# Ten Strassen pairs of feed-forward blocks, token differences by GpSimd, and the last product by token halves with the final norm between

## The chip, the cores and the metric

The kernel runs on one NeuronCore of a Trainium2 chip. TensorE (PE) multiplies, VectorE (DVE) and ScalarE (ACT) do elementwise work and may read PSUM, GpSimd (POOL) does elementwise work between SBUF tiles, and SyncE's queue (SP) issues nearly all DMAs. The engines run at the same time, each takes its own instructions in a fixed order, and they wait for one another through semaphores. The metric is device time in microseconds (us), the median of several executions; one more execution was taken with the hardware profiler, and all the rows below come from it.

## The reference

A trunk of two layers over 640 tokens (512 of a prompt, 8 x 16 of samples), width 1024. Each layer adds to the residual `x` a mixer (pooling and differential attention in layer 0, an RWKV-7 recurrence in layer 1), a cross attention, and a feed-forward block. Only the feed-forward block and the last norm are touched here:

```python
def swiglu(h, wg, wu, wd):
    return (jax.nn.silu(h @ wg) * (h @ wu)) @ wd
# in each layer
h = rmsnorm(x, P['norm_ffn_g'][l])
x = x + swiglu(h, P['ffn_wg'][l], P['ffn_wu'][l], P['ffn_wd'][l])
# after both layers
y = rmsnorm(x, P['final_norm_g'])
```

`wg` and `wu` are 1024 x 2816, `wd` is 2816 x 1024.

## The kernel before

The residual lies with the width on the partitions: eight tiles `x[0..7]` of 128 x 640. An fp32 product is made of three matmuls on split operands: `split` (L216) rounds a tile to a high part (a cast on ScalarE) and takes the low part as the difference (a subtraction on VectorE, out of the source and the high part), and high x high, high x low and low x high are added up in PSUM. Every weight goes the same way: a DMA brings it into a raw tile (`wr` in `load_w`, `wraw` in `strassen`), ScalarE casts it to `wh`, VectorE makes `wl`. There are two tiles `wr` and three each of `wh` and `wl`. All elementwise helpers are single lines (`tt` is L211, `stt` L214, `mm` L230), so the profile tells instructions apart by their tiles.

The 2816 hidden columns are 22 blocks of 128. One block of gate and up takes 2 weights x 8 contraction blocks x 3 terms x 2 halves of 320 tokens = 96 matmuls of 320 columns. `ffn` (L1036) does blocks 0 and 1 straight from `x` (`un`, the tokens' factor `rstd` is multiplied in behind PSUM). While they run it makes the normed tiles `ys` (`xf` in the profile), and their splits `hl` (`xn`). Blocks 2 and 3 are computed from `hl` as whole products; during them VectorE makes, in place, the token differences of Strassen's scheme between the left half `L` and the right half `R` of the tokens (16 subtractions of 128 x 320 in `ys`) and their splits: `c` (`xc`: T2 and T4), `d` (`xd`: T3), and T1, which goes into the right halves of `hl[0..3]`. Then `wd` for blocks 0 to 3, and three groups of six blocks, each of three Strassen pairs and a `wd` product of six blocks.

`strassen` (L1126) computes two blocks with seven products of 24 matmuls, 168 in place of 192. It loads four raw weight tiles (A11, A12, A21, A22), makes S1, S2 and two differences in place (the rows `wraw<-wraw`), and splits seven of them. Products are accumulated in PSUM banks `p_a` (0 to 3) and `p_b` (4 to 7), which the blocks before it also used.

`final` (L2012) comes behind the last `wd` product. For each of five tiles of 128 tokens it transposes eight tiles of `x` into two banks, squares them with row sums on ScalarE, makes the factor, multiplies on VectorE and writes out.

The order of the instructions on each engine is set when the program is built, by a scheduler that plays the program through a timeline of its own: an instruction written later can stand ahead of an earlier one, and the semaphore waits follow from that order.

Of the kernel before, what the change touches and what calls it, by code (L numbers as in the profile page):

```python
# [9 lines left out]
F32 = mybir.dt.float32  # L10
F32R = mybir.dt.float32r
AF = mybir.ActivationFunctionType
ALU = mybir.AluOpType
# [4 lines left out]
D = 1024  # L18
# [3 lines left out]
NT = NP + NB * TS  # L22
NF = 22
HALVES = ((0, 320), (320, 320))
# [15 lines left out]
class Trunk:  # L40
# [995 lines left out]
    def ffn(self, l):  # L1036


        nc, io = self.nc, self.io
        self.banks(g=(0, 1, 2, 3, 4, 5), r=(6, 7))  # L1040
        wg, wu, wd = io["ffn_wg"][l], io["ffn_wu"][l], io["ffn_wd"][l]
        gcol = self.col["norm_ffn_g"][:, 8 * l:8 * l + 8]
        un = self.normed(gcol)
        first = [[self.load_w(self.wview(w, 0, 8, 0, 128), 8, 128)] for w in (wg, wu)]
        _, rstd = self.rms("r")
        r0 = rstd[0]
        L, R = slice(0, 320), slice(320, 640)

        hida = self.hl(2, "hid")
        with self.scope():  # L1050
            for f in range(2):
                sg, pr = self.t("sgate", 1)[:, 0:NT], self.t("gate")[:, 0:NT]

                def ev_g(m, pts):
                    for p, (t0, n) in zip(pts, HALVES):
                        self.tt(sg[:, t0:t0 + n], p, r0[:, t0:t0 + n])
                        self.act(sg[:, t0:t0 + n], sg[:, t0:t0 + n], AF.Silu)

                def ev_u(m, pts):
                    for p, (t0, n) in zip(pts, HALVES):  # L1060
                        self.tt(pr[:, t0:t0 + n], p, r0[:, t0:t0 + n])
                    self.tt(pr, pr, sg)
                    self.split(hida[f], pr)

                self.gemm(un, wg, 128, ev_g, c0=f * 128, first=() if f else first[0])
                self.gemm(un, wu, 128, ev_u, c0=f * 128, first=() if f else first[1])
                if f == 0:
                    ys = self.blocks(8, "xf")
                    hl = self.hl(8, "xn")
                    for k in range(8):  # L1070
                        self.stt(ys[k], self.x[k], gcol[:, k:k + 1], r0)
                        self.split(hl[k], ys[k])
        self.give(un, rstd)
        hidb = self.hl(2, "hid")
        c, d = self.hl(4, "xc"), self.hl(2, "xd")
        with self.scope():

            for k in range(4):
                y1, y2 = ys[k], ys[4 + k]
                self.tt(y1[:, L], y1[:, R], y1[:, L], ALU.subtract)  # L1080
                self.tt(y1[:, R], y2[:, R], y1[:, R], ALU.subtract)
                self.tt(y2[:, R], y2[:, R], y1[:, L], ALU.subtract)
                self.tt(y2[:, L], y2[:, L], y2[:, R], ALU.subtract)
                self.split(c[k], y2)
                self.split([t[:, (L, R)[k % 2]] for t in d[k // 2]], y1[:, R])
            for f in (2, 3):
                sg, pr = self.t("sgate", 1)[:, 0:NT], self.t("gate")[:, 0:NT]

                def ev_g(m, pts):
                    for p, (t0, n) in zip(pts, HALVES):  # L1090
                        self.act(sg[:, t0:t0 + n], p, AF.Silu)

                def ev_u(m, pts):
                    for p, (t0, n) in zip(pts, HALVES):
                        self.tt(pr[:, t0:t0 + n], p, sg[:, t0:t0 + n])
                    self.split(hidb[f - 2], pr)
# [7 lines left out]
        self.give(hida, hidb)  # L1104
        part = lambda h, s: (h[0][:, s], h[1][:, s])
        rhs = dict(B11=[part(hl[k], L) for k in range(4)], T1=[part(hl[k], R) for k in range(4)],
                   B21=[part(hl[4 + k], L) for k in range(4)], B22=[part(hl[4 + k], R) for k in range(4)],
                   T2=[part(c[k], R) for k in range(4)], T3=[part(d[k // 2], (L, R)[k % 2]) for k in range(4)],
                   T4=[part(c[k], L) for k in range(4)])
        for f0, nf in ((4, 6), (10, 6), (16, 6)):  # L1110
            self.banks(a=(0, 1, 2, 3), b=(4, 5, 6, 7), g=(4, 5, 6, 7), r=(6, 7))
            hid = self.hl(nf, "hid")

            at = dict(A11=0, A21=1, A22=2, A12=3, S1=4, S2=5)
            with self.scope():
                for f in range(0, nf, 2):
                    self.strassen(wg, wu, f0 + f, rhs, hid[f:f + 2], at)
                    at = dict(A21=at["A11"], A22=at["S2"], A11=at["S1"], A12=at["A21"], S1=at["A12"], S2=at["A22"])
            if f0 == 16:
                self.give(hl, c, d)  # L1120
                if l == 0:
                    self.mem = self.mem_parts("r")
            self.gemm(hid, wd, 1024, self.add_x, r0=f0 * 128)
            self.give(hid)

    def strassen(self, wg, wu, f, rhs, hid, at):  # L1126

# [881 lines left out]
            self.tt(o, p[:, 0:nch * 64], o)  # L2009


    def final(self):  # L2012
        nc, io = self.nc, self.io
        with self.scope():
            gb = [self.t("gb")[:, 0:512] for _ in range(2)]
            for g in range(2):
                nc.sync.dma_start(out=gb[g], in_=io["final_norm_g"][g * 512:(g + 1) * 512].partition_broadcast(128))
            for i in range(5):
                dst = io["y_prompt"][0, i * 128:(i + 1) * 128, :] if i < 4 else io["y_sample"].rearrange("b t d -> (b t) d")
                pg = []  # L2020
                ss = self.s("fss", 2)
                for g in range(2):
                    p = self.ps()
                    for j in range(4):
                        self.tr(p[:, j * 128:(j + 1) * 128], self.x[g * 4 + j][:, i * 128:(i + 1) * 128], 128)
                    pg.append(p)
                    sq = self.t("fsq")[:, 0:512]
                    self.act(sq, p, AF.Square, accum=ss[:, g:g + 1])
                rt = self.s("frt")
                self.tt(rt, ss[:, 0:1], ss[:, 1:2], ALU.add)  # L2030
                self.act(rt, rt, AF.Sqrt, scale=1.0 / D, bias=self.epsc[:, 0:1])
                nc.vector.reciprocal(rt, rt)
                for g in range(2):
                    y = self.t("y", 4)[:, 0:512]
                    self.stt(y, pg[g], rt, gb[g])
                    nc.sync.dma_start(out=dst[:, g * 512:(g + 1) * 512], in_=y)

    def run(self):
        self.banks(g=range(8))
        self.memd = [(self.dr.tile([128, 8, 256], F32, name=f"memk{l}"), self.dr.tile([128, 2, 1024], F32, name=f"memv{l}")) for l in range(2)]  # L2040
        self.load_x()
        with self.scope():
            self.constants()
        self.turn_x()
        self.even()
        self.cross(0)
        self.ffn(0)
        self.rwkv()
        self.cross(1)
        self.ffn(1)  # L2050
        self.final()


INS = ['x_prompt', 'x_sample', 'cache_diff_k', 'cache_diff_v', 'state_pool', 'state_rw_shift', 'state_rw_wkv',
# [33 lines left out]
```

## Time and profile before

| | |
|---|---|
| median of 3 runs | 2333.88 us (2332.62 to 2336.47) |
| the profiled execution, its own time | 2334.3 us |
| its span, first to last instruction | 2332.5 us |
| granted TensorE clock, mean over the span | 0.961 of full speed |
| busy: PE, DVE, ACT, POOL | 2204.8, 1407.1, 978.8, 338.2 us |

Busy time is the time in which an engine has at least one instruction under way. Matmuls overlap, so a matmul that the profile shows as 309 ns long may follow the last one after less than half of that: what a row of matmuls costs is the length of the stretch that they fill, divided by their number. The clock is given as a share of full speed: 1.00 is 2.4 GHz and 0.50 is 1.2 GHz.

### The profile page before, as it was taken

What the parts mean: (1) busy time and instruction counts of PE and PEld (TensorE: products, weight loads), DVE (VectorE), ACT (ScalarE), POOL (GpSimd) and SP (SyncE); (2) the same over time, 40 slices, a digit from 0 to 9 for tenths busy, and PEclk for the clock granted to TensorE, in tenths of its full rate; (3) what the DMA queues carried; (4) which work ended last, traced back from release to release, by engine and by line L of the source; (5) the groups of instructions that cost most, each with busy time, mean ns of one, the idle gap of its engine ahead of it and who ended that gap; (6) DMA issues with size and microseconds to landing.
All of it is one profiled execution on the core that took longest, in us unless ns stands there. A gap on an engine that the chain in (4) does not pass through costs nothing. (4 is left out here: it accounts for less than half of the span.)

```text
span 2332.5 us, 45975 instructions
## 1 busy us (share of the span) xinstructions
PE 2204.8 (95%) x18781; PEld 2054.9 (88%) x18781; DVE 1407.1 (60%) x2403; ACT 978.8 (42%) x1917; POOL 338.2 (14%) x392
## 2 busy tenths in 40 slices
PE   7999899999999999998998987888999999999997
PEld 7886799888999999998887886666998899999997
DVE  4458443456775656576668977457534596757573
ACT  4335432334443434456755352356323353525252
POOL 0113120002000000135452111223200110000000
PEclk8999999999999999999998887798999999999999
DMA  5228554532123232354237677674345222323222
GB/s 157 82 68 277 168 159 154 164 118 73 55 73 91 74 90 73 108 176 123 80 90 182 168 178 185 181 212 132 115 133 172 76 86 64 100 64 100 73 64 73
DMA packets 428483, 280.43 MB, mean 120 GB/s; under 512 B 79289, under 2 KB 383694, under 8 KB 428273
## 3 DMA queue, kind: packets, MB, share of 16 engines
q1 hardware_dynamic: 424673, 268.01, 39.6%
q0 software_dynamic: 3600, 9.49, 1.2%
q8 instruction: 148, 2.42, 0.4%
q14 instruction: 62, 0.51, 0.1%
HBM read 231.22 MB, written 46.20 MB: 119 GB/s over the span
## 5 line engine op out<-in xcount | busy, mean ns | idle before, releaser
L247 ACT CAST wh<-wr 128x1024 fp32r<-128x1024 f32 (+3 forms) x223 | 199.9, 898 | 459.1 <-PE p_g L230 370.6
L230 PE MATMUL p_g<-xn,wh 128*128 128x320 f32 x1408 | 291.4, 314 | 1.4 <-DVE xn L214 0.7
L230 PE MATMUL p_g<-hid,wh 128*128 128x320 f32 x1408 | 267.7, 309 | 0.8 <-DVE memhl L211 0.8
L211 DVE TENSOR_TENSOR x<-x,p_g 128x320 f32<-128x320 f32 x224 | 99.6, 483 | 238.3 <-PE p_g L230 238.0
L211 DVE TENSOR_TENSOR wl<-wr,wh 128x1024 fp32r<-128x1024 f32 (+2 forms) x195 | 204.2, 1048 | 62.1 <-ACT wh L247 49.1
L230 PEld LDWEIGHTS p_g<-xn,wh 128*128 128x128 f32 x1408 | 228.4, 190 | 10.7 <-issue 8.4
L230 PEld LDWEIGHTS p_g<-hid,wh 128*128 128x128 f32 x1408 | 221.8, 188 | 1.3 <-DVE memhl L211 1.0
L211 DVE TENSOR_TENSOR wl<-wraw,wh 128x1024 fp32r<-128x1024 f32 x126 | 154.1, 1223 | 108.1 <-ACT wh L220 90.6
L220 ACT CAST wh<-wraw 128x1024 fp32r<-128x1024 f32 x126 | 132.5, 1051 | 164.8 <-PE p_a L230 79.7
L230 PE MATMUL p_a<-xn,wh 128*128 128x320 f32 x864 | 191.3, 309 | 0.0
L230 PE MATMUL p_g<-xn,wl 128*128 128x320 f32 x704 | 182.7, 313 | 4.5 <-DVE wl L211 4.5
L230 PE MATMUL p_g<-hid,wl 128*128 128x320 f32 x704 | 163.2, 309 | 0.0
L230 PEld LDWEIGHTS p_a<-xn,wh 128*128 128x128 f32 x864 | 144.8, 188 | 0.0
L230 PE MATMUL p_g<-mixr,wh 128*128 128x320 f32 (+2 forms) x640 | 133.4, 317 | 7.9 <-ACT mv L198 3.6
L230 PE MATMUL p_a<-xn,wl 128*128 128x320 f32 x432 | 133.0, 309 | 0.0
L230 PEld LDWEIGHTS p_g<-xn,wl 128*128 128x128 f32 x704 | 123.6, 190 | 8.4 <-DVE wl L211 4.9
L230 PEld LDWEIGHTS p_g<-hid,wl 128*128 128x128 f32 x704 | 118.5, 188 | 0.0
L230 PE MATMUL p_g<-xohl,wh 128*128 128x320 f32 x512 | 111.5, 323 | 6.7 <-ACT xohl L220 6.6
L230 PEld LDWEIGHTS p_g<-mixr,wh 128*128 128x128 f32 (+2 forms) x640 | 101.1, 182 | 17.4 <-issue 5.4
L230 PEld LDWEIGHTS p_g<-xohl,wh 128*128 128x128 f32 x512 | 84.6, 193 | 10.4 <-ACT xohl L220 8.9
L211 DVE TENSOR_TENSOR wraw<-wraw 128x1024 f32<-128x1024 f32 x72 | 87.4, 1221 | 1.0
L230 PE MATMUL p_g<-mixr,wl 128*128 128x320 f32 (+2 forms) x320 | 82.0, 317 | 0.0
(532 smaller groups left out, 4976.1 us busy)
## 6 DMA issues: line engine op xcount, KB each, us to landing
wraw<-in_ffn_wg SPq DMA_DIRECT2D x72, 256.0 KB
wraw<-in_ffn_wu SPq DMA_DIRECT2D x72, 256.0 KB
wr<-in_ffn_wd SPq DMA_DIRECT2D x48, 384.0 KB
kc<-in_cache_mem_k SPq DMA_DIRECT2D x64, 256.0 KB
vc<-in_cache_mem_v SPq DMA_DIRECT2D x64, 256.0 KB
wr<-in_ev_w_in SPq DMA_DIRECT2D x16, 512.0 KB
wr<-in_xa_wk SPq DMA_DIRECT2D x16, 512.0 KB
vc<-in_cache_diff_v SPq DMA_DIRECT2D x32, 256.0 KB
```

The lines of the kernel that those rows point to most:

```text
L211: (eng or self.nc.vector).tensor_tensor(out, a, b, op=op)
L220: self.nc.scalar.copy(hi, src)
L230: self.nc.tensor.matmul(out, lhsT, rhs, start=start, stop=stop, **kw)
L247: nc.scalar.copy(wh[0:rows, 0:n], wr[0:rows, 0:n])
```

## The change

- Ten pairs: the whole products of blocks 2 and 3 are gone, and these blocks are the first Strassen pair. The groups are now blocks 0 to 5 (0 and 1 as before, two pairs), 6 to 11, 12 to 17 and 18 to 21 (two pairs), each with its `wd` product: 6, 6, 6 and 4 blocks in place of 4, 6, 6 and 6.
- The 16 token differences of a layer go to GpSimd (`sub`, with `eng=nc.gpsimd`), and the splits of `c` are made by halves of 320 columns. `hl[0..3]` get only their left halves at first.
- In layer 1 the last `wd` product (4 blocks) is `last_down`: its weights are split once into 16 tiles (`wd` in the rows) and kept, the product is made for tokens 0 to 383, all eight output tiles, and then for tokens 384 to 639. The final norm of token tiles 0, 1 and 2 stands between the output tiles of the second pass, that of tiles 3 and 4 behind it. It has four banks of its own (`p_o`), and `final` becomes `final_gain` and `final_tile`.

```diff
@@ ffn
                     for k in range(8):
                         self.stt(ys[k], self.x[k], gcol[:, k:k + 1], r0)
-                        self.split(hl[k], ys[k])
+                        self.split([t[:, L] for t in hl[k]] if k < 4 else hl[k], ys[k][:, L] if k < 4 else ys[k])
...
-            for k in range(4):
-                y1, y2 = ys[k], ys[4 + k]
-                self.tt(y1[:, L], y1[:, R], y1[:, L], ALU.subtract)
-                self.tt(y1[:, R], y2[:, R], y1[:, R], ALU.subtract)
-                self.tt(y2[:, R], y2[:, R], y1[:, L], ALU.subtract)
-                self.tt(y2[:, L], y2[:, L], y2[:, R], ALU.subtract)
-                self.split(c[k], y2)
-                self.split([t[:, (L, R)[k % 2]] for t in d[k // 2]], y1[:, R])
-            for f in (2, 3):
...
-                self.gemm(hl, wg, 128, ev_g, c0=f * 128)
-                self.gemm(hl, wu, 128, ev_u, c0=f * 128)
+        sub = lambda o, a, b: self.tt(o, a, b, ALU.subtract, eng=nc.gpsimd)
+        for k in range(4):
+            y1, y2 = ys[k], ys[4 + k]
+            sub(y1[:, L], y1[:, R], y1[:, L])
+            sub(y1[:, R], y2[:, R], y1[:, R])
+            sub(y2[:, R], y2[:, R], y1[:, L])
+            self.split([t[:, R] for t in c[k]], y2[:, R])
         for k in range(4):
             self.split((hl[k][0][:, R], hl[k][1][:, R]), ys[k][:, L])
+        for k in range(4):
+            y1, y2 = ys[k], ys[4 + k]
+            sub(y2[:, L], y2[:, L], y2[:, R])
+            self.split([t[:, (L, R)[k % 2]] for t in d[k // 2]], y1[:, R])
+            self.split([t[:, L] for t in c[k]], y2[:, L])
         self.give(ys)
-        self.gemm(hida + hidb, wd, 1024, self.add_x)
...
-        for f0, nf in ((4, 6), (10, 6), (16, 6)):
+        for f0, nf in ((0, 6), (6, 6), (12, 6), (18, 4)):
...
+            done = hida if f0 == 0 else []
+            new = self.hl(nf - len(done), "hid")
+            hid = done + new
...
+                if l == 1:
+                    self.last_down(hid, wd, f0)
+                    return
+    def last_down(self, hid, wd, f0):
+        nc = self.nc
+        self.banks(g=(4, 5, 6, 7), o=(0, 1, 2, 3))
+        nb = len(hid)
+        ws = [self.take(2, "wd", dt=F32R) for _ in range(8)]
...
+            def half(m, t0, n):
+                p = self.ps("g")
...
+                        self.mm(p[:, 0:n], w[m][a][:, k, :], hid[k][x][:, t0:t0 + n], start=(i == 0), stop=(i == 3 * nb - 1))
...
+                self.tt(self.x[m][:, t0:t0 + n], self.x[m][:, t0:t0 + n], p[:, 0:n], ALU.add)
+
+            for m in range(8):
+                wr = self.wtile("wr", F32)[:, 0:nb * 128]
+                nc.sync.dma_start(out=wr.rearrange("p (k m) -> p k m", k=nb), in_=self.wview(wd, f0 * 128, nb, m * 128, 128))
+                parts = [t[:, 0:nb * 128] for t in ws[m]]
+                self.split(parts, wr)
+                w.append([t.rearrange("p (k m) -> p k m", k=nb) for t in parts])
+                half(m, 0, 384)
+            for m in range(8):
+                half(m, 384, 256)
+                if m in (1, 3, 5):
+                    self.final_tile(m // 2, gb)
+            for i in (3, 4):
+                self.final_tile(i, gb)
```

What the scheduler makes of it, at the three places that matter. First VectorE in layer 1, from the factor `rstd` of the norm on. The kernel before:

```order
L200 COPY rstd<-p_r 128x320
L211 TENSOR_TENSOR sgate<-p_g,rstd 128x320 x2
L214 SCALAR_TENSOR_TENSOR xf<-x,ct,rstd 128x640 x8
L211 TENSOR_TENSOR gate<-p_g,rstd 128x320 x2
L211 TENSOR_TENSOR wl<-wr,wh 128x1024
L211 TENSOR_TENSOR xn<-xf,xn 128x640 x8
L211 TENSOR_TENSOR gate<-gate,sgate 128x640
L211 TENSOR_TENSOR wl<-wr,wh 128x1024
L211 TENSOR_TENSOR xf<-xf 128x320 x4
L211 TENSOR_TENSOR gate<-p_g,rstd 128x320 x2
```

And the changed kernel, the stretch in which the first pair's operands are made, up to the last one that its product with T2 needs (the second `xc` pair at the end is `c[1]`; `e_21442` and `e_21443` are the first pair's gate and up, taken out of `p_b`):

```order
L211 TENSOR_TENSOR gate<-gate,sgate 128x640
L211 TENSOR_TENSOR xc<-xf,xc 128x320 x2
L211 TENSOR_TENSOR wl<-wraw,wh 128x1024
L211 TENSOR_TENSOR xc<-xf,xc 128x320
L211 TENSOR_TENSOR e_21442<-e_21442,p_b 128x320
L211 TENSOR_TENSOR xc<-xf,xc 128x320
L211 TENSOR_TENSOR hid<-gate,hid 128x640
L211 TENSOR_TENSOR xc<-xf,xc 128x320 x2
L211 TENSOR_TENSOR wl<-wraw,wh 128x1024
L211 TENSOR_TENSOR e_21443<-e_21443,p_b 128x320
L211 TENSOR_TENSOR xc<-xf,xc 128x320 x2
```

The subtractions `xf<-xf` are gone from this queue; what stood behind two whole blocks of matmuls (the splits of `xc`) now stands among the first pair's own weights (`wl<-wraw`) and results.

Second, GpSimd, the same place, with the numbers of the tiles (`xf_21191` to `xf_21198` are `ys[0]` to `ys[7]`), the first nine of the sixteen:

```order
L211 TENSOR_TENSOR xf_21191<-xf_21191 128x320
L211 TENSOR_TENSOR xf_21192<-xf_21192 128x320
L211 TENSOR_TENSOR xf_21193<-xf_21193 128x320
L211 TENSOR_TENSOR xf_21191<-xf_21195,xf_21191 128x320
L211 TENSOR_TENSOR xf_21194<-xf_21194 128x320
L211 TENSOR_TENSOR xf_21192<-xf_21196,xf_21192 128x320
L211 TENSOR_TENSOR xf_21193<-xf_21197,xf_21193 128x320
L211 TENSOR_TENSOR xf_21195<-xf_21195,xf_21191 128x320
L211 TENSOR_TENSOR xf_21194<-xf_21198,xf_21194 128x320
```

None of them stood in this queue before. Each writes over its input, so the first of a tile waits until that tile's split has been read.

Third, TensorE at the end of the program, from the last `wd` product of the changed kernel on (before, 40 transposes in one row stood behind all matmuls):

```order
L230 MATMUL p_g<-hid,wd 128x384 x22
L230 MATMUL p_g<-hid,wd 128x256 x24
L227 MATMUL p_o<-ident,x 128x128 x5
L230 MATMUL p_g<-hid,wd 128x256 x24
L227 MATMUL p_o<-ident,x 128x128 x7
L230 MATMUL p_g<-hid,wd 128x256 x24
L227 MATMUL p_o<-ident,x 128x128 x8
L230 MATMUL p_g<-hid,wd 128x256 x24
L227 MATMUL p_o<-ident,x 128x128 x16
```

So 24 of the 40 transposes have moved ahead of the last matmuls (four more stand just above these rows), and 16 stay behind them.

## Rows read from the trace of the kernel before

**Rows 1.** The page, the span and section 1: busy time of the engines.

```profile
span 2332.5 us, 45975 instructions
...
PE 2204.8 (95%) x18781; PEld 2054.9 (88%) x18781; DVE 1407.1 (60%) x2403; ACT 978.8 (42%) x1917; POOL 338.2 (14%) x392
```

**Rows 2.** Stretches of layer 1's feed-forward block and of the end; the columns are in the first row.

```profile
core 0: us, PE busy (x) PEld busy (x) DVE busy (x) ACT busy (x) POOL busy (x), PEclk, DMA share, GB/s
1878.30:1908.50 30.20, 30.18 (x205) 29.57 (x204) 24.74 (x35) 15.92 (x22) 1.73 (x1) 1.00 0.29 84
1908.50:1938.00 29.50, 29.50 (x204) 29.50 (x203) 24.68 (x48) 13.80 (x26) 0.00 (x0) 1.00 0.19 54
...
2156.00:2198.00 42.00, 42.00 (x288) 42.00 (x287) 20.56 (x30) 8.10 (x10) 0.00 (x0) 1.00 0.20 56
...
2319.30:2332.50 13.20, 4.87 (x24) 3.55 (x24) 7.19 (x17) 4.66 (x15) 0.00 (x0) 0.65 0.53 199
```

**Rows 3.** Timeline of the end: start, length, engine; last matmuls, transposes, last output.

```profile
2313.32 0.46 PE L230 MATMUL p_g<-hid,wl 128*128 128x320 f32 x2
2313.62 1.91 PE L227 MATMUL p_g<-ident,x 128*128 128x128 f32 x16
2319.39 3.55 PE L227 MATMUL p_g<-ident,x 128*128 128x128 f32 x16 [3.86 <-DVE y L214]
...
2327.39 0.15 DVE L211 TENSOR_TENSOR frt<-fss 128x1 f32<-128x1 f32 x1
...
2328.16 1.41 DVE L214 SCALAR_TENSOR_TENSOR y<-p_g,frt,gb 128x512 f32<-128x512 f32 x2
```

**Rows 4.** Timeline, PE: three matmuls of 256 columns, one after the other.

```profile
299.76 0.40 PE L230 MATMUL p_g<-wh,memhl 128*128 128x256 f32 x2
300.00 0.28 PE L230 MATMUL p_g<-wl,memhl 128*128 128x256 f32 x1
300.11 0.40 PE L230 MATMUL p_g<-wh,memhl 128*128 128x256 f32 x2
```

**Rows 5.** Timeline, VectorE in layer 1's block, before its Strassen pairs.

```profile
1892.96 0.49 DVE L200 COPY rstd<-p_r 128x320 f32<-128x320 f32 x1 [3.71 <-PE p_r L230]
...
1894.37 6.45 DVE L214 SCALAR_TENSOR_TENSOR xf<-x,ct,rstd 128x640 f32<-128x640 f32 x8
...
1902.66 5.96 DVE L211 TENSOR_TENSOR xn<-xf,xn 128x640 fp32r<-128x640 f32 x8
...
1910.42 1.69 DVE L211 TENSOR_TENSOR xf<-xf 128x320 f32<-128x320 f32 x4
1912.03 0.88 DVE L211 TENSOR_TENSOR gate<-p_g,rstd 128x320 f32<-128x320 f32 x2
...
1956.33 3.62 DVE L211 TENSOR_TENSOR wraw<-wraw 128x1024 f32<-128x1024 f32 x3
```

**Rows 6.** Timeline in layer 0's norm: GpSimd and VectorE side by side.

```profile
560.80 1.60 POOL L211 TENSOR_TENSOR acc<-acc,sq 128x640 f32<-128x640 f32 x1 [2.72 <-ACT sq L208]
560.87 0.88 DVE L211 TENSOR_TENSOR x<-x,p_g 128x320 f32<-128x320 f32 x2
561.67 1.82 DVE L211 TENSOR_TENSOR wl<-wr,wh 128x1024 fp32r<-128x1024 f32 x1
...
563.38 1.57 POOL L211 TENSOR_TENSOR acc<-acc,sq 128x640 f32<-128x640 f32 x1 [0.98 <-ACT sq L208]
563.41 2.23 DVE L214 SCALAR_TENSOR_TENSOR xn<-x,ct,xn 128x640 fp32r<-128x640 f32 x1
```

**Rows 7.** Groups of GpSimd, shapes apart: count, busy us, mean ns, idle before.

```profile
L211 POOL TENSOR_TENSOR acc<-acc,sq 128x640 f32<-128x640 f32 x30 | 54.0, 1800 | 156.6 <-ACT sq L208 137.8 <-DMA wr<-in_xa_wo 18.7
...
L211 POOL TENSOR_TENSOR vb<-vb,bon 128x512 f32<-128x512 f32 x10 | 11.4, 1136 | 102.0 <-DMA vb<-d_v 96.3 <-DVE tr L211 5.3 <-PE p_x L227 0.4
```

**Rows 8.** Timeline, a weight of 512 KB: issue on SP, then ScalarE's cast of it.

```profile
1872.78 0.37 SPq L245 DMA_DIRECT2D wr<-in_ffn_wu  x1
...
1876.63 1.05 ACT L247 CAST wh<-wr 128x1024 fp32r<-128x1024 f32 x1 [0.41 <-DMA wr<-in_ffn_wu]
```

More of the change, by code (lines that the diff above doesn't have):

```diff
@@ L1123, in ffn @@
             self.gemm(hid, wd, 1024, self.add_x, r0=f0 * 128)
-            self.give(hid)
+            self.give(new)
+            if f0 == 0:
+                self.give(hida)
+    def last_down(self, hid, wd, f0):
[3 more added lines that the diff above has]
+        ws = [self.take(2, "wd", dt=F32R) for _ in range(8)]
+        w = []
+        with self.scope():
+            gb = self.final_gain()
+            def half(m, t0, n):
+                p = self.ps("g")
+                i = 0
+                for k in range(nb):
+                    for a, x in ((0, 0), (0, 1), (1, 0)):
+                        self.mm(p[:, 0:n], w[m][a][:, k, :], hid[k][x][:, t0:t0 + n], start=(i == 0), stop=(i == 3 * nb - 1))
+                        i += 1
+                self.tt(self.x[m][:, t0:t0 + n], self.x[m][:, t0:t0 + n], p[:, 0:n], ALU.add)
[12 more added lines that the diff above has]
+                self.final_tile(i, gb)
@@ L2009, in y_gate @@
             self.tt(o, p[:, 0:nch * 64], o)
-    def final(self):
-        nc, io = self.nc, self.io
[L2014 to L2036, printed above, removed]
@@ new lines, in final_gain, with final_tile @@
+    def final_gain(self):
+        gb = [self.t("gb")[:, 0:512] for _ in range(2)]
+        for g in range(2):
+            self.nc.sync.dma_start(out=gb[g], in_=self.io["final_norm_g"][g * 512:(g + 1) * 512].partition_broadcast(128))
+        return gb
+    def final_tile(self, i, gb):
+        nc, io = self.nc, self.io
+        dst = io["y_prompt"][0, i * 128:(i + 1) * 128, :] if i < 4 else io["y_sample"].rearrange("b t d -> (b t) d")
+        pg = []
+        ss = self.s("fss", 2)
+        for g in range(2):
+            p = self.ps("o")
+            for j in range(4):
+                self.tr(p[:, j * 128:(j + 1) * 128], self.x[g * 4 + j][:, i * 128:(i + 1) * 128], 128)
+            pg.append(p)
+            sq = self.t("fsq")[:, 0:512]
+            self.act(sq, p, AF.Square, accum=ss[:, g:g + 1])
+        rt = self.s("frt")
+        self.tt(rt, ss[:, 0:1], ss[:, 1:2], ALU.add)
+        self.act(rt, rt, AF.Sqrt, scale=1.0 / D, bias=self.epsc[:, 0:1])
+        nc.vector.reciprocal(rt, rt)
+        for g in range(2):
+            y = self.t("y", 4)[:, 0:512]
+            self.stt(y, pg[g], rt, gb[g])
+            nc.sync.dma_start(out=dst[:, g * 512:(g + 1) * 512], in_=y)
@@ L2050, in run @@
         self.ffn(1)
-        self.final()
 INS = ['x_prompt', 'x_sample', 'cache_diff_k', 'cache_diff_v', 'state_pool', 'state_rw_shift', 'state_rw_wkv',
```

19 lines of the change are left out of this document (3 added, 16 removed).

## The prediction

> **What bounds the kernel now.** First the page: TensorE has something under way in 2204.8 of 2332.5 us [rows 1], so it is the engine to follow; but such a share is a mean over stages, and the stages that the change touches have to be looked at by themselves. The windows of layer 1's feed-forward block show TensorE without a gap at the full clock: 30.18 of 30.20 us for blocks 0 and 1, 29.50 of 29.50 for blocks 2 and 3, 42.00 of 42.00 for a `wd` product [rows 2]. In these stages a matmul removed is time removed, and a wait added is time added. The same rows show how thin the cover is at the block's beginning: VectorE is busy for 24.74 and 24.68 of those first two stretches. The end is different: from 2319.3 us TensorE is busy 4.87 of 13.20 us at a mean clock of 0.65, and a chain of small steps of the final norm sets the time.
>
> The prices. A matmul of 320 columns costs 42.00 / 288 = 0.146 us, as 288 of them fill a stretch. Three of 256 columns take 300.11 - 299.76 = 0.35 us, 0.118 each [rows 4]; on the line through these two points one of 384 columns costs 0.174.
>
> **Matmuls.** A pair of blocks as whole products is 192 matmuls, as a Strassen pair 168. One pair a layer changes over: 24 x 0.146 = 3.5 us a layer, **-7.0 us** for both. The `wd` products only change their grouping (22 blocks either way), which costs nothing: all are TensorE at full density.
>
> **The end.** Now 2332.5 - 2313.8 = 18.7 us lie behind the last product's last matmul [rows 3]. Afterwards 24 transposes stand inside the second pass, at 1.91 / 16 = 0.119 us each: 2.9 us of TensorE. Behind the last matmul remain the addition to `x` (0.5), 16 transposes (1.9), the last square with its sum (0.8), the steps from sum to factor (2328.16 - 2327.39 = 0.8), two outputs (1.4), and from the end of the last output to the span's end 2332.5 - 2329.6 = 2.9: 8.3 us. With the 2.9 that is 11.2 and a gain of 7.5; I take 7.0, for waits between the steps. The passes themselves cost as much as before: 96 x 0.174 + 96 x 0.118 = 28.0 us, against 192 x 0.146 = 28.0. But in the first pass a weight is wanted every 12 x 0.174 = 2.1 us, and all eight come through the two tiles `wr`. A load of twice the size takes 1876.63 - 1872.78 = 3.85 us from issue to cast [rows 8]; with cast and split (0.6 and 0.7, half of the rows for 1024 columns) a tile turns in at most 5.1 us, so a weight comes every 2.6 us at worst: 0.5 us late for each of five (the order has three splits ahead of the product). Between 0 and 2.5 I take 1.0. The end gives **-6.0 us**.
>
> **The beginning of each block.** This decides. Whole products of blocks 2 and 3 needed no token difference and gave VectorE 28 us to make them. Now Strassen's first pair stands directly behind block 1, from 1908.5 us on in the trace's time. In the built order TensorE first does the products with B21, B11 and T3, 72 matmuls, 10.5 us, and could start on the one with T2 (differences `c`) at 1919.0 and end it at 1922.5.
>
> What VectorE has to do by then, read from its order: from the factor `rstd` on (1892.96 in the rows, about 1894.4 for the first instruction behind it, as seven matmuls and a weight sum now stand ahead) until the last split of `c[1]`, there are 8 products `xf` (6.45 us as a row), 8 instructions of 640 columns (5.96, as a row of 8), 6 of 1024 (twice 3.62), 20 of 320 columns between SBUF tiles (5 x 1.69) and 10 of 320 out of PSUM (5 x 0.88) [rows 5]: 6.5 + 6.0 + 7.2 + 8.5 + 4.4 = 32.5 us, all back to back, to 1926.9. Behind that split 16 of T2's 24 matmuls are left, 2.3 us. So even with GpSimd's part for nothing, T2 ends at 1929.2 in place of 1922.5: 6.7 us late, or 5 if the overlap of neighbouring instructions, which the lengths of the rows hold at each end, is taken out.
>
> GpSimd's part is not for nothing. Rows 6 show the two engines side by side. GpSimd adds two SBUF tiles from 560.80 to 562.40; an addition on VectorE out of PSUM beside it keeps its 0.44 us, but the weight split that starts at 561.67 takes 1.82 us where it takes 1.21 by itself; and the product that starts at 563.41, just behind GpSimd's next addition, takes 2.23 where it takes 0.81 to 0.88, ending 0.7 us after GpSimd does. VectorE, with both inputs in SBUF, has waited for GpSimd's instruction to end, and its cost has been added on, not hidden. The Trainium skill, "SBUF — State Buffer", section "SBUF: two separate sides", makes this a rule: one port pair is shared, held for a whole instruction, and a VectorE instruction with two SBUF inputs and a GpSimd instruction shut each other out. By that rule the subtractions are added to VectorE's queue in full; if the engines ran freely beside each other, the sum below would come out near the first rival's 2333 us. The trace agrees with the rule, with those 0.6 and 1.35 us lost.
>
> The price of one: no row has GpSimd at 320 columns. Half of the undisturbed 1.57 us for 640 is 0.785; the bounds are 0.71 (1136 ns x 320/512) and 0.90 (half of the mean 1800, which holds waits) [rows 6, 7]. Sixteen make 12.6 us (11.4 to 14.4). VectorE had paid 16 x 0.42 = 6.8 us for the same work; moving it costs more of the same resource than it frees. Of the 12.6 up to 2.6 can lie beside the six PSUM instructions that come after GpSimd's start (each subtraction writes over what is being split, so GpSimd starts late). ScalarE hides nothing: its casts of `c` wait for GpSimd's last steps, and behind them in its queue stand the cast of A21 and the copies that free `p_a`. So T2 ends 5 + 10.0 to 6.7 + 12.6 = 15 to 19 us late. I take 16.0, near the low end since the lower figure for VectorE alone is the cleaner one, and 0.5 for the next pair's first weight, whose load waits until S1 has been split, late now (0 to 2). Later pairs have slack: in the three pairs that follow one another now TensorE never waits.
>
> Per layer: -3.5 + 16.5 = +13.0; **+26.0 us** for both blocks. Sum: 26.0 - 6.0 = +20.0. The profiled execution took 2334.3 us (span 2332.5), 0.4 over the median 2333.88: **2354.3 us**.
>
> **Rivals.** First, **GpSimd runs beside VectorE**. For it: only shapes of 640 columns are shown above, and GpSimd waits for several things and may find VectorE idle or at PSUM. Against it: rows 6, and VectorE's list without idle time. Then each block is 5 to 7 us late, net +1.5 to +3.5, both +3 to +7, and with the end -6.0: 2331 to 2335 us, which can't be told from no change.
>
> Second, **everything stays covered**, and it is faster: the last split of `c[1]` is done by 1920.2 (when a third of T2 has run). VectorE would have to get 6.7 us ahead of its list with GpSimd free, 17 without. For it: the kernel before fills the same stretch without one wait of TensorE, with more subtractions on VectorE. Against it: it had 28 us more of matmuls to do so. Price: -7.0 - 6.0, 2321 us.
>
> Third, worse: **a starved TensorE also loses its clock**. In rows 3, after a wait of 3.86 us, 16 transposes take 3.55 us where 16 took 1.91, with a mean clock of 0.65 in that stretch. A product of 24 at half the clock takes 3.5 us more; as VectorE would be the one waited for anyway, most is absorbed, and I count 0 to 2.5 us a block, in the range only. That the change doesn't do what it says I leave out: the order shows the two blocks gone and the transposes moved. The instructions between the two blocks keep their work, though the tiles that they get differ; 5 us either way.
>
> **How the numbers follow.** A change below 0.2% (4.7 us) can't be told from none. Forecast: 0.71, with stalls of 13 to 19.5 us a block, a clock loss and the 5 us elsewhere: 2341 to 2364. First rival 0.16; second 0.13. The range must leave out no more than 2 in 10: dropping the second rival and what lies above, it is 2330 to 2363. Slower by over 0.2% is 0.71, within 0.2% 0.15, faster 0.14 (the second rival, and the lower edge of the first).
>
> **What would show it.** TensorE's waits, none in the feed-forward block now, should appear in the first pair of each layer, 13 to 19 us in all, released by VectorE and ScalarE, at the first product (banks not yet emptied) and at `xd` and `xc`. VectorE's 320-column splits there should grow from 0.42 us to about 1.2 wherever GpSimd is busy, and GpSimd's subtractions, with their waits for the port, to over 0.8. The end behind the last matmul should be 8 to 10 us. I am wrong if the splits keep their 0.42 us, or if TensorE goes from block 1 into the first pair without waits.

## The result, and the profile after

Device time of the changed kernel is 2372.88 us (2365.48 to 2375.30), of the kernel before 2333.25 us on the same chip: ratio 1.016 with a 95% interval of 1.0145 to 1.0175, 39.6 us slower. The forecast was 2354.3 (2330 to 2363): the sign was right, the size half of what came. A second set of runs (e1 below) gave 2376.42 against 2335.52, ratio 1.0169 (1.0151 to 1.0188).

The profiled execution took 2365.5 us, the lowest of the four, and has a span of 2363.7. Top of its page, against [rows 1]:

```profile
span 2363.7 us, 45983 instructions
...
PE 2199.6 (93%) x18733; PEld 2047.3 (87%) x18733; DVE 1420.0 (60%) x2405; ACT 989.2 (42%) x1943; POOL 387.6 (16%) x424
```

TensorE is busy 5.2 us less and the span is 31.2 us longer: work went, waits came. The first table to make is one by stages, cut at the first gate matmul and the last `wd` matmul of each feed-forward block. "Others with the same order" are the traces of the experiments in which that stage has the instruction order of the kernel before: e6 to e12 up to layer 0's block and for the mixer, the same without e8 for layer 0's block; for layer 1's block and the end e8 alone, whose matmuls are those of the kernel before.

| stage, us | before | others with the same order | changed | changed again (e1) |
|---|---|---|---|---|
| to layer 0's feed-forward block | 564.5 | 561.2 to 566.7 | 560.2 | 561.2 |
| layer 0's block | 440.7 | 440.6 to 442.7 | 462.4 | 462.7 |
| layer 1's mixer and cross attention | 873.2 | 862.9 to 872.9 | 877.5 | 881.7 |
| layer 1's block | 435.4 | 435.8 | 453.9 | 452.7 |
| behind the last product's last matmul | 18.75 | 18.74 | 9.66 | 9.65 |

Means of the changed kernel less means of the order before: +20.6, +11.2, +17.7 and -9.1, together +40.4. The stretch ahead of the first changed instruction has the same order in all of them and was 4.2 us shorter in the mean of the changed kernel's two traces, so these traces show 36 us in all, and the medians 39.6 and 40.9: both profiled executions of the changed kernel were the lowest of their four, 7 us below the median, and what the others took longer for is in no trace. The first profile alone shows 31.2, as the mixer before happened to be at the long end of its spread of 10 us.

**The first pair.** Windows of layer 1's block in the changed kernel; they answer to [rows 2] (the columns are the same):

```profile
1900.10:1933.10 33.00, 30.99 (x208) 29.89 (x206) 29.85 (x41) 16.46 (x24) 7.68 (x3) 1.00 0.17 49
1933.10:1950.60 17.50, 7.53 (x48) 7.04 (x48) 16.06 (x19) 7.11 (x14) 17.50 (x15) 0.79 0.10 30
1950.60:1960.30 9.70, 7.09 (x25) 6.69 (x26) 8.07 (x13) 4.96 (x12) 2.52 (x2) 0.50 0.37 108
1960.30:1970.00 9.70, 9.70 (x68) 9.70 (x67) 5.82 (x6) 4.92 (x8) 0.00 (x0) 1.00 0.01 3
```

In the second stretch TensorE is busy 7.53 of 17.50 us while VectorE is busy 16.06 and GpSimd all of it; in the third the clock is at 1.2 GHz (0.50). From 1960.3 us on all is as before. TensorE's rows there, with the wait and its releaser in brackets:

```profile
1933.69 0.53 PE L230 MATMUL p_b<-xn,wh 128*128 128x320 f32 x2 [1.60 <-DVE sgate L211]
...
1950.67 1.44 PE L230 MATMUL p_b<-xd,wh 128*128 128x320 f32 x4 [9.44 <-ACT wh L220]
1954.65 0.63 PE L230 MATMUL p_a<-xc,wh 128*128 128x320 f32 x1 [2.54 <-ACT xc L220]
1955.08 0.47 PE L230 MATMUL p_b<-xd,wl 128*128 128x320 f32 x1
1955.35 0.73 PE L230 MATMUL p_b<-xd,wh 128*128 128x320 f32 x2
```

Three waits, 13.6 us, and matmuls behind them that follow each other after 0.27 us in place of 0.146; layer 0 has the same three (1.63, 9.43, 2.54). The longest one is released by ScalarE, but ScalarE is only the messenger. Its rows ahead of that cast of A21:

```profile
1946.76 0.46 ACT L220 CAST xc<-xf 128x320 fp32r<-128x320 f32 x1 [1.68 <-POOL xf L211]
1949.22 0.46 ACT L220 CAST xc<-xf 128x320 fp32r<-128x320 f32 x1 [2.00 <-POOL xf L211]
1949.58 1.04 ACT L220 CAST wh<-wraw 128x1024 fp32r<-128x1024 f32 x1
```

The cast itself waited for nothing (it has no bracket); it stands in ScalarE's queue behind two casts of `c` that wait for GpSimd. And why GpSimd is late, in the rows of GpSimd and VectorE of the same timeline:

```profile
1927.94 5.93 POOL L211 TENSOR_TENSOR xf<-xf 128x320 f32<-128x320 f32 x1 [22.20 <-DVE xn L211]
...
1939.83 1.91 DVE L211 TENSOR_TENSOR wl<-wraw,wh 128x1024 fp32r<-128x1024 f32 x1
1941.66 1.14 DVE L211 TENSOR_TENSOR xd<-xf,xd 128x320 fp32r<-128x320 f32 x1
...
1942.42 2.17 POOL L211 TENSOR_TENSOR xf<-xf 128x320 f32<-128x320 f32 x2
...
1943.80 3.27 DVE L211 TENSOR_TENSOR xd<-xf,xd 128x320 fp32r<-128x320 f32 x3
...
1953.39 0.47 DVE L211 TENSOR_TENSOR e<-e,p_b 128x320 f32<-128x320 f32 x1
1953.79 0.48 DVE L211 TENSOR_TENSOR xc<-xf,xc 128x320 fp32r<-128x320 f32 x1
```

While both have work, they take turns: a split of 320 columns is 1.14 us long where it is 0.48 after GpSimd's last subtraction (1953.1 us), and each subtraction 1.1. All sixteen took 25.2 us, 1927.9 to 1953.1.

**Layer 0's last product** has 192 matmuls now, 288 before, and the 16 transposes of the memory for the next layer stand inside it in both. By the price of full density (0.146 us) it should have become 14.0 us shorter; it went from 46.7 (the window of 46.24 below, and three of its matmuls that stand ahead of it) to 40.51, and to 38.82 in e1: 6 to 8 us were lost. Its window in the kernel before (columns of [rows 2]):

```profile
958.86:1005.10 46.24, 44.53 (x305) 43.63 (x304) 19.03 (x34) 15.26 (x25) 9.97 (x6) 1.00 0.47 148
```

and in the changed kernel:

```profile
982.13:1022.64 40.51, 35.35 (x212) 33.13 (x211) 17.88 (x35) 14.20 (x26) 9.74 (x6) 0.87 0.51 161
```

The rows of its timeline in which it was lost, TensorE's and SyncE's issue of a load:

```profile
990.91 0.60 PE L227 MATMUL p_r<-ident,mt 128*128 128x128 f32 x4
...
991.43 0.80 SPq L852 DMA_DIRECT2D mt<-in_mem_prompt  x2
...
994.80 1.48 PE L227 MATMUL p_r<-ident,mt 128*128 128x128 f32 x4 [3.29 <-DMA mt<-in_mem_prompt]
...
998.60 0.90 PE L230 MATMUL p_g<-hid,wh 128*128 128x320 f32 x2 [0.49 <-DVE memhl L211]
```

The load of the next memory tiles goes out only when the transposes at 990.91 have read the last ones (the same `mt` buffers), and the order has no matmul between them and the transposes that need the load; 3.3 us of it lie bare, and what follows runs at half the clock (0.50 from 994.8 to 1000.0 us). The kernel before has 31 matmuls of the product there. Its issue of the same load, and the first transposes of it:

```profile
964.68 0.83 SPq L852 DMA_DIRECT2D mt<-in_mem_prompt  x2
...
969.41 0.38 PE L227 MATMUL p_r<-ident,mt 128*128 128x128 f32 x2
```

Its longest wait in this product was 0.92 us. The shorter product did not run out of matmuls to put there: 144 of its 192 stand behind the last transpose (216 of 288 before). The scheduler laid the transposes otherwise: the last eight stand behind 48 matmuls of the product, with none between them and the eight before; in the kernel before they stand behind 67 to 72, and the last of the eight before behind 36.

**The mixer** computes the same and stands in another order. The loss lies in one stretch of it, from the recurrence's last `p_l` matmul to the first output product: 132.9 to 137.5 us in the eight traces of the old order, 148.6 and 151.8 in the changed kernel. Rows of the changed kernel's timeline there, in the order of the chain (SyncE, GpSimd, VectorE, TensorE):

```profile
1561.87 2.56 SPq L1995 DMA_DIRECT2D vb<-d_v  x4
...
1565.37 1.06 POOL L211 TENSOR_TENSOR vb<-vb,bon 128x512 f32<-128x512 f32 x1 [17.22 <-DMA vb<-d_v]
...
1567.80 1.53 DVE L211 TENSOR_TENSOR yl<-yl,vb 128x512 f32<-128x512 f32 x1 [4.88 <-POOL vb L211]
1569.25 0.47 DVE L1938 TENSOR_SCALAR zs<-p_x,sel 128x256 f32<-128x256 f32 x1
...
1570.85 1.12 PE L230 MATMUL p_x<-trs,wcs 128*64 128x64 f32 x16 [7.81 <-DVE gmean L1985]
```

VectorE's addition of `vb` to an output stands ahead of the `zs` rows that empty the `p_x` banks, and `vb` was asked for late: TensorE stops for 7.8 us (8.3 in e1). The profile names `gmean` as the releaser, a row of VectorE right behind the `zs` rows. The kernel before has its additions of `vb` in that stretch without a wait.

**The end** is what was forecast, against [rows 3]:

```profile
2350.93 3.09 PE L230 MATMUL p_g<-hid,wd 128*128 128x256 f32 x24
...
2353.85 1.91 PE L227 MATMUL p_o<-ident,x 128*128 128x128 f32 x16
...
2359.28 1.41 DVE L214 SCALAR_TENSOR_TENSOR y<-p_o,frt,gb 128x512 f32<-128x512 f32 x2
2360.06 0.99 SPq L2064 DMA_DIRECT2D out_y_sample<-y  x2
```

### The profile page after: what moved, and what is told of

Its sections match the earlier page's. It is cut to its first block, busy times and chain, and to the rows that moved or that the text cites. A ratio compares the mean times of both kernels' runs of the same rounds, so it can differ in the third digit from the quotient of the medians.

```text
span 2363.7 us, 45983 instructions
## 1 busy us (share of the span) xinstructions
PE 2199.6 (93%) x18733; PEld 2047.3 (87%) x18733; DVE 1420.0 (60%) x2405; ACT 989.2 (42%) x1943; POOL 387.6 (16%) x424
## 5 line engine op out<-in xcount | busy, mean ns | idle before, releaser
L230 PE MATMUL p_g<-hid,wh 128*128 128x320 f32 x1280 | 245.9, 311 | 0.8 <-DVE memhl L211 0.5
L230 PE MATMUL p_g<-xn,wh 128*128 128x320 f32 x1152 | 243.1, 315 | 2.3 <-DVE xn L214 1.6
L211 DVE TENSOR_TENSOR wl<-wraw,wh 128x1024 fp32r<-128x1024 f32 x140 | 173.5, 1240 | 112.7 <-ACT wh L220 107.9
L211 DVE TENSOR_TENSOR x<-x,p_g 128x320 f32<-128x320 f32 (+2 forms) x224 | 100.2, 483 | 221.8 <-PE p_g L230 221.7
L230 PE MATMUL p_a<-xn,wh 128*128 128x320 f32 x960 | 212.1, 309 | 0.0
L230 PEld LDWEIGHTS p_g<-hid,wh 128*128 128x128 f32 x1280 | 203.9, 190 | 1.8 <-DVE memhl L211 0.9
L230 PEld LDWEIGHTS p_g<-xn,wh 128*128 128x128 f32 x1152 | 187.8, 190 | 11.8 <-issue 8.4
L230 PE MATMUL p_g<-xn,wl 128*128 128x320 f32 x576 | 152.9, 314 | 4.5 <-DVE wl L211 4.5
L230 PEld LDWEIGHTS p_g<-xn,wl 128*128 128x128 f32 x576 | 101.9, 190 | 8.4 <-DVE wl L211 4.9
L230 PE MATMUL p_b<-xd,wh 128*128 128x320 f32 x320 | 73.0, 324 | 18.9 <-ACT wh L220 18.9
```

The costliest lines, as they stand in the source:

```text
L211: (eng or self.nc.vector).tensor_tensor(out, a, b, op=op)
L230: self.nc.tensor.matmul(out, lhsT, rhs, start=start, stop=stop, **kw)
```

## The experiments

Theory A is the prediction's: VectorE and GpSimd take turns, and the first pair starves. The rivals have letters as they come.

**e1. The changed kernel again.**

> The changed kernel once more, with a second profile. It separates what belongs to the feed-forward block from what varies between executions: the first profiled execution took 2365.5 us, the three others 2372.8 to 2375.3. Theory A (the first pair starves, as forecast): 14 to 15 us of waits of TensorE and 2.5 to 3 us at half the clock in the first pair of each layer again, to within 0.5 us, and the 7 us more lie outside the feed-forward blocks, in the mixers and cross attention. Theory B (the starvation itself varies, and was only lucky in the first profile): waits of 18 us or more a layer in this one. Time by either: 2366 to 2376 us, ratio to the kernel before 1.014 to 1.018.

2376.42 us, ratio 1.0169. The waits in the first pair are the same to 0.02 us (1.61, 9.46 and 2.55 in layer 1), the block of layer 1 is 1.3 us shorter than in the first profile and the mixer 4.3 longer. A, not B: the block repeats itself, and what varies lies outside it.

**e2. The differences on VectorE.**

```diff
-        sub = lambda o, a, b: self.tt(o, a, b, ALU.subtract, eng=nc.gpsimd)
+        sub = lambda o, a, b: self.tt(o, a, b, ALU.subtract)
```

> The changed kernel with the 16 differences a layer on VectorE again, nothing else. Theory A (VectorE and GpSimd shut each other out on SBUF operands, so GpSimd's 0.7 to 0.8 us each are added on): VectorE pays 16 x 0.42 = 6.8 us in place of the 11 to 12.6 us that GpSimd's cost it, the waits of the first pair fall from 14.4 to about 10 us a layer, and the time by 8 us, to about 2364. Rival C (GpSimd does no harm, the cover is all that is missing): VectorE has 6.8 us more to do, the waits grow to 19 to 21 us a layer, time about 2384. Rival D (what counts is only the order in which the scheduler puts the first products): within 3 us of the changed kernel.

2359.19 us, ratio 1.0096 (1.0079 to 1.0114): 17 us faster than e1, twice what A expected. By stages 6.4 and 5.9 us less in the two blocks, and 3.3 in the mixer, whose order came out differently again. The timeline of e2, TensorE's waits in layer 1's first pair:

```profile
1928.70 0.54 PE L230 MATMUL p_b<-xn,wh 128*128 128x320 f32 x2 [1.61 <-DVE sgate L211]
1940.30 0.41 PE L230 MATMUL p_b<-xd,wh 128*128 128x320 f32 x1 [4.07 <-DVE xd L211]
1949.07 0.86 PE L230 MATMUL p_a<-xn,wh 128*128 128x320 f32 x4 [2.53 <-ACT wh L220]
```

and of VectorE beside the second of them:

```profile
1939.77 0.48 DVE L211 TENSOR_TENSOR xd<-xf,xd 128x320 fp32r<-128x320 f32 x1
1940.17 0.88 DVE L211 TENSOR_TENSOR xf<-xf 128x320 f32<-128x320 f32 x2
```

8.2 us of waits in place of 13.6, though VectorE does sixteen subtractions more; its splits are back at 0.48. C falls, as the waits shrink where it wanted them to grow, and D falls as the only cause. But the engine was not the only thing that changed: in e2 ScalarE casts A21 ahead of all splits of `c`, in the changed kernel behind two of them, so this run by itself doesn't say how much of the 6 us a layer is the engine and how much the order. e5 and e11 bear on that.

**e3. No differences at all** (`sub` does nothing, so the splits take undifferenced tiles).

> The changed kernel without the 16 differences (the splits read the normed tiles as they are, so the feed-forward result is another one); VectorE's own list is unchanged and GpSimd does nothing here. It measures what the differences cost in all. Theory A: 5 to 6.7 us of waits a layer remain from VectorE's own list, about 10 us a layer are gone with some of the half clock: 2350 to 2355 us. Rival C (the differences lie beside VectorE's work for nothing): waits stay at 12 us or more a layer, time 2366 or more.

2352.20 us, ratio 1.0075 (1.0059 to 1.009), inside A's numbers. Two waits are left in layer 0's first pair (3.65 and 1.66 us) and one in layer 1's (its row of the timeline):

```profile
1931.07 0.54 PE L230 MATMUL p_b<-xn,wh 128*128 128x320 f32 x2 [3.62 <-DVE sgate L211]
```

So VectorE's own list leaves 3.6 to 5.3 us of waits, more than the 3.5 us of matmuls that the pair saves: with the differences free of charge, ten pairs would still not gain. Layer 1's block took 440.9 us here, with nine pairs and the same end 437.8 (e4) and 439.1 (e7).

**e4. Nine pairs and the new end**: blocks 2 and 3 whole, differences on VectorE, and `last_down`.

```diff
-        self.gemm(hida + hidb, wd, 1024, self.add_x)
-        for f0, nf in ((4, 6), (10, 6), (16, 6)):
+        for f0, nf in ((0, 6), (6, 6), (12, 6), (18, 4)):
```

> The kernel before (blocks 2 and 3 as whole products, nine pairs, differences on VectorE under their cover) with only the new end: groups of 6, 6, 6 and 4 blocks, the last product by token halves with the norm of tiles 0 to 2 between. Theory A: the end is worth 6 us by itself, 2327 us, ratio 0.9975, with 9 to 10 us behind the last matmul and no wait of TensorE in either pass; the order of the mixer may move that by 4 us. Rival E (the end's gain is eaten by waits for its weights in the first pass): within 1 us of the kernel before.

2345.55 us, ratio 1.004 (1.0023 to 1.0056): 10 us slower than the kernel before where 6 faster was expected, by neither theory. This run found what the prediction had missed. Tail and layer 1 are as A has them (10.35 us behind the last matmul, block 437.8 with 2.9 of transposes in it, no wait), but layer 0's block, whose matmuls are those of the kernel before, takes 449.8 in place of 440.7, and the mixer 883.0. Layer 0's last product in e4:

```profile
977.15:1016.43 39.28, 34.13 (x212) 32.10 (x211) 17.88 (x35) 14.19 (x26) 9.75 (x6) 0.91 0.53 165
```

**e5. Layer 0 grouped 4, 6, 6, 6** in the changed kernel, so that its last product has 288 matmuls.

```diff
-        for f0, nf in ((0, 6), (6, 6), (12, 6), (18, 4)):
+        for f0, nf in (((0, 4), (4, 6), (10, 6), (16, 6)) if l == 0 else ((0, 6), (6, 6), (12, 6), (18, 4))):
```

> The changed kernel (ten pairs, GpSimd's differences), with layer 0's blocks grouped 4, 6, 6, 6 as in the kernel before, so that its last product has 288 matmuls again and not 192; layer 1 as in the changed kernel. In five traces the last product of layer 0, with the transposes of the memory inside it, took 46.6 us at 288 matmuls (41.8 is the price of such a product by itself) and 39.1 to 40.8 us at 192 (28.1 by itself): 4.8 us against 11 to 12.6 lost to transposes, their DMA and the clock. Theory F (the shorter product is too short a cover for the loads of the memory): 6 to 8 us faster than the changed kernel, about 2368 in this set of runs (e1: 2376), and the wait for the memory's load under 1 us. Rival G (the transposes cost the same wherever they stand): no change, 2376.

2356.45 us against 2332.12, ratio 1.0096 (1.0074 to 1.0117), some 17 us better than e1, where F expected 6 to 8. F's own term is there at its low end: the wait for the memory's load is gone, and layer 0's block went from 462.6 to 456.8 (5.8 us). F's reason is not borne out: with 288 matmuls the transposes stand again where the kernel before has them, with 31 matmuls under the second load, and the product of 192 had 144 to spare. It is the order that came back. Two waits for VectorE remain in the timeline of that product:

```profile
984.42 0.77 PE L227 MATMUL p_r<-ident,mt 128*128 128x128 f32 x4 [0.92 <-DVE memhl L211]
986.96 0.90 PE L230 MATMUL p_g<-hid,wh 128*128 128x320 f32 x2 [1.76 <-DVE memhl L211]
```

The rest came where none was expected, both by order: the mixer took 871.2 us (8.4 less), and in layer 1's first pair A21's split stands ahead of those of `c` now, so its waits are 1.55, 4.80, 2.82 and 0.33, 9.5 us in place of 13.6, and the block is 3.4 us shorter (layer 0 keeps 13.6). Rival D has that much right: with GpSimd's differences still in place, A21's split ahead of `c` gives 3.4 of the 5.9 us that e2 gained in layer 1, and 2.5 are left for the engine.

**e6. Layer 0 as before, layer 1 as changed.**

```diff
     def ffn(self, l):
+        if l == 0:
+            return self.ffn_first(l)
```

(`ffn_first` is the `ffn` of the kernel before.)

> Layer 0's feed-forward block as in the kernel before, layer 1's as in the changed kernel (ten pairs, GpSimd's differences, new end). The stages of the traces add up to: layer 1's block with the new end 453 to 454 us against 435.4, the tail 9.7 against 18.75, so +9.4 by these, and the mixer between 0 and +8 according to its order and its jitter: 2343 to 2351 against 2335. Theory A expects waits of 14.5 us in the first pair; rival H (the loss sits mostly in layer 0 and in the mixer's new order, layer 1 gains): under 2337.

2338.27 us, ratio 1.0022 (1.001 to 1.0034): 6.2 slower, between A and H. With layer 0 as before the scheduler gives the mixer exactly its old order, and it takes 864.6 us. Layer 1's block is 454.1 and the waits are 1.61, 9.42 and 2.55 again. The stages give +9.7, some 3.5 us more than the medians; what that is was not found, and it is less than the mixer's spread.

**e7 and e12. Layer 0 as before, layer 1 with nine pairs and the new end** (e4's `ffn` behind the same two lines as in e6).

> Layer 0's feed-forward block as in the kernel before, and in layer 1 nine pairs (blocks 2 and 3 whole, differences on VectorE) with groups of 6, 6, 6 and 4 and the new end: the new end without the shorter last product of layer 0, which cost 9.2 us in e4. Theory F: 6 us faster than the kernel before, 2326 to 2332, ratio 0.996 to 0.999, with the last product of layer 0 at 46 to 47 us. Rival I (what e4 lost lies in the mixer's order, not in layer 0's last product): 2338 or more.

2325.22 us, ratio 0.9969 (0.9956 to 0.9983). Again:

> The best version so far (e7: layer 0 as before, layer 1 with nine pairs and the new end) again, beside e10 on the same chip: 6 to 7 us faster than the kernel before, ratio 0.996 to 0.998.

2328.67 us, ratio 0.9983 (0.9973 to 0.9994). F's time holds and I's does not, though I names a part of it: layer 1's block has the same order in e4 and e7, and e4's loss was layer 0's block with its last product (7.9 us) and the order of the mixer that came with it (14.6, both against the means of the order before). The end alone gains 5.5 to 6.9 us, 9.1 behind the last matmul less 3.6 inside layer 1's block, and this version is faster than both kernels.

**e8. The kernel before with its differences on GpSimd**, under the cover of blocks 2 and 3.

```diff
-                self.tt(y1[:, L], y1[:, R], y1[:, L], ALU.subtract)
+                self.tt(y1[:, L], y1[:, R], y1[:, L], ALU.subtract, eng=nc.gpsimd)
```

(the other three likewise)

> The kernel before with only the 16 differences of each layer moved to GpSimd; blocks 2 and 3 stay whole products, 28 us of cover. It measures the two engines' contention where TensorE does not wait for it. Theory A: VectorE's 320-column splits between SBUF tiles take 0.8 to 1.2 us beside a running GpSimd, as one and one they alternate, in place of 0.42 to 0.48 us; GpSimd's first subtraction waits for some us while VectorE goes from one such instruction to the next, the others take 1.1 us each; TensorE's waits in the block stay under 1 us, time within 3 us of the kernel before. Rival C (the engines run beside each other): splits at 0.48 us, GpSimd's subtractions at 0.7 to 0.8.

2333.12 us, ratio 1.0003 (0.9986 to 1.002); no wait of TensorE in layer 1's block. GpSimd and VectorE in the timeline of layer 0:

```profile
592.36 5.97 DVE L211 TENSOR_TENSOR xn<-xf,xn 128x640 fp32r<-128x640 f32 x8
593.26 7.67 POOL L211 TENSOR_TENSOR xf<-xf 128x320 f32<-128x320 f32 x1 [22.33 <-DVE xn L211]
598.24 0.82 DVE L211 TENSOR_TENSOR gate<-gate,sgate 128x640 f32<-128x640 f32 x1
598.98 1.22 DVE L211 TENSOR_TENSOR wl<-wr,wh 128x1024 fp32r<-128x1024 f32 x1
600.89 4.46 POOL L211 TENSOR_TENSOR xf<-xf 128x320 f32<-128x320 f32 x5
603.12 0.66 DVE L211 TENSOR_TENSOR xd<-xf,xd 128x320 fp32r<-128x320 f32 x1 [2.92 <-ACT xd L220]
603.70 0.88 DVE L211 TENSOR_TENSOR gate<-p_g,rstd 128x320 f32<-128x320 f32 x2
604.50 1.93 DVE L211 TENSOR_TENSOR wl<-wr,wh 128x1024 fp32r<-128x1024 f32 x1
```

The contention is all there (`wl` 1.93 in place of 1.22, the two products out of PSUM untouched at 0.88) and costs nothing under 28 us of matmuls.

**e9. e6 with the differences on VectorE** (e2's edit).

> Layer 0's feed-forward block as in the kernel before; layer 1 with ten pairs and the new end, its 16 differences on VectorE: e6 with one thing changed. By e2, where layer 1's block came from 453.3 (mean of two traces) to 447.4 us, it should be 6 us faster than e6 and equal to the kernel before or 2 us under it; waits of the first pair 8 to 9 us in place of 14.4. Rival C (GpSimd does no harm): e6's time or more.

2335.77 us, ratio 1.0015 (1.0004 to 1.0027). Layer 1's block went from 454.1 to 445.9 (8.2 us), the waits to 7.5 (1.61, 4.07, 1.82), with A21's cast moved ahead as in e2; the medians differ by less, 0.0007 of the time or 1.6 us where 6 were expected, with intervals of some 2.7 us to either side, so by the times alone it can't be told from e6.

**e10. e9 with the `wd` product of blocks 0 and 1 as a cover**, ahead of the first pair.

```diff
-        for f0, nf in ((0, 6), (6, 6), (12, 6), (18, 4)):
+        self.banks(a=(0, 1, 2, 3), b=(4, 5, 6, 7), g=(4, 5, 6, 7), r=(6, 7))
+        self.gemm(hida, wd, 1024, self.add_x)
+        self.give(hida)
+        for f0, nf in ((2, 6), (8, 6), (14, 4), (18, 4)):
```

> As e9, and the wd product of blocks 0 and 1 (96 matmuls, 14.0 us) stands alone between block 1 and the first pair, as a cover that costs no matmul; the groups of layer 1 are then 2, 6, 6, 4, 4 blocks. It puts 16 additions of 0.42 us more on VectorE there (6.7 us) and half of these behind the list if the order puts them late. Theory J (only the cover is missing): the waits of the first pair fall from 8 to 9 us to 0 to 3, and with 3.5 us fewer matmuls it is level with nine pairs (e7, 2325) or up to 3 us faster. Rival K (VectorE's additions eat the cover): waits of 5 us or more, slower than e7 by 2 us or more.

2339.60 us, ratio 1.0017 (1.0002 to 1.0032): nothing gained over e9, 11 us slower than e12. K, by another way than its additions: the pair hardly waits any more (0.68 us), but the cover does, as its own operand `hid` is made by the same engines behind the same list. Its waits of over 1 us come to 8.0, as much as the pair's in e9 (7.5). The two longest in e10's timeline:

```profile
1921.38 1.41 PE L230 MATMUL p_g<-hid,wh 128*128 128x320 f32 x4 [3.61 <-ACT hid L220]
1924.98 0.90 PE L230 MATMUL p_g<-hid,wh 128*128 128x320 f32 x2 [2.19 <-DVE hid L211]
```

**e11. e10 with GpSimd's differences.**

> As e10 with the differences on GpSimd: whether the cover is enough for that too. Theory A (shut-out): VectorE's list is 4 to 8 us longer than in e10, of which the cover takes what it has left: waits of 2 to 8 us, 2 to 7 us slower than e10. Rival C: level with e10 or faster.

2342.26 us, ratio 1.0039 (1.0025 to 1.0053): 2.7 us slower than e10, and layer 1's block 5.1 longer (454.2 against 449.2). A. TensorE's order in layer 1's block is the same in these two, those of VectorE and ScalarE are not, so this is the closest that the runs come to the engine by itself.

## Why the prediction was right in its main term and wrong in its sum

- **Matmuls, -3.5 us a layer**: right; TensorE has 48 matmuls less (18733 in place of 18781), 24 a layer, it is busy 5.2 us less in all, and a product of the same number of matmuls costs the same to 0.3 us.
- **The beginning of each block, +16.5 a layer**: right. The 336 matmuls of the first group's two pairs take 64.7 us in layer 0 and 65.1 in layer 1; at full density (0.1467 each, as the first two pairs of the kernel before have them) they are 49.3. With the wait of 1.6 ahead of them that is 17.0 and 17.4 a layer. It is made up otherwise: 13.6 of waits, at the low edge of the 13 to 19, and 3.5 of half clock, which the prediction had counted as 0 to 2.5, in the range only. That a starved TensorE loses its clock was no rival of the waits but a part of them.
- **GpSimd and VectorE in turn**: right in kind. The rule of the Trainium skill ("SBUF — State Buffer", section "SBUF: two separate sides") holds in these traces: splits of 0.48 us take 1.14 beside GpSimd and instructions out of PSUM keep their length. e3 puts all that the differences cost on GpSimd at 9.6 us in layer 0 and 12.4 in layer 1 (whole block, e1 and the first profile against e3), with 10 to 12.6 in the sum. How much of that comes from the choice of GpSimd is less sure, as no run changes the engine and keeps the order of all queues: e2 is 6 us a layer better, of which e5 gives 3.4 to the place of A21's split in layer 1 and leaves 2.5; e11 against e10, with TensorE's order the same, has 5.1. VectorE's own lateness, 5 to 6.7 by the sum, was 3.6 to 5.3.
- **The end, -6.0**: right. 9.1 us less behind the last matmul, less 2.9 of transposes and 0.7 more inside layer 1's block: 5.5 by the stages of e7 and e12, whose blocks of layer 1 take 439.1 and 439.3.
- **"The `wd` products only change their grouping (22 blocks either way), which costs nothing"**: this step failed. It counted matmuls and not what stands inside the last product of layer 0: loads, transposes and splits of the next layer's memory. With 192 matmuls the scheduler laid these otherwise, and a load that had 31 matmuls beside it had none: 3.3 us of wait and the half clock behind it, about 7 us in all (layer 0's 20.6 less 13.5), much the same in e4 with nine pairs (9.2 and 7.9 against the kernel before and the mean of its order). The cover was not used up, 144 matmuls stand behind; why the scheduler put the transposes there was not found.
- **"The instructions between the two blocks keep their work ... 5 us either way"**: this failed too, by 11 us. Where the scheduler met another layer 0 it laid the mixer's instructions otherwise; five changed layers 0 gave five orders, with 871 to 883 us, and the old layer 0 the old order, with 862.9 to 873.2 in eight traces. e6 to e12 bring order and time back together; the tiles that the instructions get come back with them, so order and tiles were not told apart, and which of the moved instructions does it was not tried on its own. Not every new order is slow: e5's 871.2 lies inside the spread of the old one. In the stretch that holds the loss e2, e3 and e4 took 145.0 to 146.5 us and e5 136.9. The chain through `vb` is one place where it shows (7.8 us of some 13 in the stretch).

27 + 7 + 11 - 5 is 40, with the medians at 39.6 and 40.9; that it fits them to 1 us is in part luck, as the traces behind it show 36 with their first stretch. Without the two failed steps the sum of 20 stands within 2 us. Both failed steps are of one kind: the change moved work that it wasn't meant to touch. The range went wrong with them: 5 us for the mixer was a guess with no row behind it, and the grouping had no bound at all. It was also narrower than its own terms: stalls of 19.5 us a block, the clock's 2.5 and the 5 elsewhere add up to 2 x (19.5 - 3.5 + 2.5) - 6.0 + 5 = +36 us, 2370, where it ends at 2363.

The first rival (GpSimd free beside VectorE) fell by e2 and e8, the second (all covered) by the waits themselves.

## What to carry to other kernels

A saving of matmuls is worth what the work behind it allows: take away a product under which other engines catch up, and ask what they had still to do (here 3.5 us saved, 17 paid). Moving elementwise work on SBUF tiles from VectorE to GpSimd gained nothing in any of these runs: it cost nothing under 28 us of matmuls (e8) and some us a layer where VectorE was the late engine; where VectorE waits, or reads PSUM, it may do better, which was not tried. And a change of grouping changes the scheduler's order in stages that it wasn't meant to touch: keep the stages that are not meant to change in their old form (e7), and compare them stage by stage before believing a total.

## What was not expected of the hardware

GpSimd does not get its turn after one of VectorE's instructions: its first subtraction lasts from 593.26 to 600.93 us in e8, through nine back-to-back instructions of VectorE with both inputs in SBUF that lose nothing, and ends once VectorE pauses (5.93 us in the changed kernel, until an instruction out of PSUM). Once it is in, the two take turns one by one, with 0.67 us for the subtraction (1.07 from one split to the next, less 0.40). With VectorE idle a subtraction took 0.84 (from 600.89 to 603.40 three of them).
